# Residual halves of some weights in a two-layer decoder trunk: ScalarE and an accumulating DMA in place of VectorE's subtraction

## Chip, cores and metric

The kernel runs on one core of a Trainium2 chip. The metric is the device time of one execution in microseconds (us). Before the change it is 1392.08 us, the median of 2 runs (1391.61 and 1392.55).

## What is computed

A decoder trunk of two layers on 256 tokens with 2048 channels, all in float32: a retention layer (8 heads), then a multi-scale causal pooling layer, then a last RMS norm.

```python
h = x                                              # (1, 256, 2048)
h = h + retention_layer(h, ret_norm, ret_w_in, ret_gn, ret_w_out)
h = h + pooling_layer(h, pool_norm, pool_w_in, pool_w_grp, pool_b_grp, pool_scale, pool_w_out)
return rms_norm(h, final_norm)

def pooling_layer(...):
    ...
    return (mix * jax.nn.silu(z)) @ w_out          # (256, 4096) @ (4096, 2048)
```

The change lies in that last product, `(mix * silu(z)) @ w_out`, alone.

## The kernel before

TensorE multiplies operands of type float32r, which keep 12 significant bits. So each float32 product a @ b is run as three: a_hi @ b_hi + a_hi @ b_lo + a_lo @ b_hi, where hi is the value rounded to float32r and lo is what the rounding leaves. Every weight therefore has to be split into hi and lo before TensorE can use it.

Weights come in units of 128 partitions x 2048 float32 (1 MB). The helper `weights` (L78 to L91) loads one unit into a tile `raw` by a DMA that SP issues (L81), and splits it in two halves of 1024 columns. For each half ScalarE writes the tile `whi` (a cast, L68) and VectorE writes the tile `wlo` (`raw` minus `whi`, L69). There are three buffers each of `raw`, `whi` and `wlo`. Half n therefore uses the `whi` and `wlo` buffers of half n-3, and ScalarE can't write `whi` of half n before TensorE has ended half n-3.

The last stage is the product with `w_out` (L432 to L487), tokens on partitions. It runs over four column blocks of 512 (`c` from 0 to 3). Each column block takes 8 units (`u` from 0 to 7), so 32 units in all, of two halves each. One half gives 12 matmuls of 512 columns: two row blocks of tokens (`t`), two blocks of channels (`j`), and three products (L442 with `whi`, L443 with `wlo`, L444 with `whi` again). They add up in two accumulators `accy`, one for each `t`. At the end of a column block, for each `t`, VectorE adds the accumulator onto the residual stream (L461), ScalarE squares the sum for the norm (L463), and GpSimd multiplies by the norm's gain (L470). The norm itself and the stores follow after the last column block.

Each engine works its own queue in order. A scheduler lays out the order when the program is built, from the program order, the buffers and its own estimates. GpSimd has little to do in this stage: the multiplications of L470, and ahead of it one load (L420). Its queue is also the one from which accumulating DMAs are issued. In the text below, the halves of an even unit are called a and b, those of the odd unit behind it c and d.

Of the kernel before, what the change touches and what calls it, by code (L numbers as in the profile page):

```python
# [7 lines left out]
F32 = mybir.dt.float32  # L8
# [3 lines left out]
ALU = mybir.AluOpType  # L12

P = 128
D = 2048
S = 256
# [8 lines left out]
EPS = 1e-6  # L25
UNIT = 2048
HALF = UNIT // 2
# [3 lines left out]
def kernel(  # L31
# [15 lines left out]
):  # L47
    """Everything lies transposed, channels on partitions and tokens on the free axis, so that no
    product's result has to be turned; only the retention's values and the last product, which the
    norm of each token follows, have tokens on partitions.  # L50

    A float32 product a @ b runs as a_hi @ b_hi + a_hi @ b_lo + a_lo @ b_hi with float32r operands,
    where hi is the value rounded to the 12 significant bits that TensorE multiplies, and lo, exact
    in float32r, is what the rounding leaves.
    """
    nc = tc.nc
# [7 lines left out]

# [1 line left out]
    def split(hi, lo, src):  # L66
        """hi and lo of src."""
        nc.scalar.copy(hi, src)  # L68
        nc.vector.tensor_tensor(out=lo, in0=src, in1=hi.bitcast(F32), op=ALU.subtract)  # L69

    def split_scaled(hi, lo, src, scale):
        """hi and lo of src times a number for each partition."""
        nc.scalar.activation(hi, src, AF.Identity, scale=scale)
        nc.vector.scalar_tensor_tensor(  # L74
            out=lo, in0=src, scalar=scale, in1=hi.bitcast(F32), op0=ALU.mult, op1=ALU.subtract
        )

    def weights(src, own=None):  # L78
        """Loads a unit of weights and splits it, in two halves, which own has room for if it is given."""
        raw = wpool.tile([P, UNIT], F32, tag="raw", name="raw", bufs=3)  # L80
        nc.sync.dma_start(out=raw, in_=src)  # L81
        halves = []
        for i in range(2):
            if own is None:
                hi = wpool.tile([P, HALF], F32R, tag="whi", name="whi")
                lo = wpool.tile([P, HALF], F32R, tag="wlo", name="wlo")
            else:
                hi, lo = own[:, i, 0], own[:, i, 1]
            split(hi, lo, raw[:, i * HALF : (i + 1) * HALF])
            halves.append((hi, lo))  # L90
        return halves  # L91

    def stationary(acc, blocks, moving):
        """acc[:, :S] + acc[:, S:] = the weights' 128 columns, transposed, times moving."""
        n = len(blocks)
        for k, (hi, lo) in enumerate(blocks):
            nc.tensor.matmul(acc, hi, moving[:, k], start=(k == 0), stop=False)  # L97
            nc.tensor.matmul(acc[:, :S], lo, moving[:, k, 0], start=False, stop=(k == n - 1))  # L98
# [4 lines left out]
    def joined(dst, acc):  # L103
        """The sum of an accumulator's halves."""
        t = ev.tile([P, S], F32, tag="hl", name="hl", bufs=2)
        nc.scalar.copy(t, acc[:, S:])
        nc.vector.tensor_tensor(out=dst, in0=acc[:, :S], in1=t, op=ALU.add)

    def column_sums(sums):
        """Adds up a [P, S] tile over its partitions; every row of the result holds the sums."""  # L110
        sp = ev.tile([P, 2, S], F32R, tag="sp", name="sp", bufs=1)
        split(sp[:, 0], sp[:, 1], sums)
        tot = ps_ret.tile([P, 512], F32, tag="ret", name="tot")
        nc.tensor.matmul(tot[:, :S], ones, sp[:, 0], start=True, stop=False)
        nc.tensor.matmul(tot[:, :S], ones, sp[:, 1], start=False, stop=True)
        return tot[:, :S]

    def rsqrt(dst, a):
        """dst = a ** -0.5, by Newton's steps from a guess on the exponent."""
        n = a.shape[-1]  # L120
        t = ev.tile([P, n], F32, tag=f"rs_t{n}", name="rs_t", bufs=1)
        nc.vector.tensor_scalar(
            out=t.bitcast(I32), in0=a.bitcast(I32), scalar1=1, scalar2=None, op0=ALU.logical_shift_right
        )
        nc.vector.tensor_scalar(
            out=dst.bitcast(I32), in0=t.bitcast(I32), scalar1=-1.0, scalar2=float(0x5F3759DF),
            op0=ALU.mult, op1=ALU.add,
        )
        if n == 1:
            nc.vector.tensor_scalar(out=a, in0=a, scalar1=-0.5, scalar2=None, op0=ALU.mult)  # L130
        for _ in range(3):
            if n == 1:
                nc.vector.tensor_scalar(out=t, in0=dst, scalar1=dst, scalar2=a, op0=ALU.mult, op1=ALU.mult)
                nc.vector.tensor_scalar(out=dst, in0=t, scalar1=1.5, scalar2=dst, op0=ALU.add, op1=ALU.mult)
                continue
            nc.vector.tensor_tensor(out=t, in0=dst, in1=dst, op=ALU.mult)
            nc.vector.scalar_tensor_tensor(out=t, in0=t, scalar=-0.5, in1=a, op0=ALU.mult, op1=ALU.mult)
            nc.vector.scalar_tensor_tensor(out=dst, in0=t, scalar=1.5, in1=dst, op0=ALU.add, op1=ALU.mult)

    def rms(dst, src, scale):  # L140
        """dst = (src * scale + EPS) ** -0.5."""
        a = ev.tile([P, S], F32, tag="rs_a", name="rs_a", bufs=1)
        nc.vector.tensor_scalar(out=a, in0=src, scalar1=scale, scalar2=EPS, op0=ALU.mult, op1=ALU.add)
        rsqrt(dst, a)
# [3 lines left out]

# [1 line left out]
    vec = const.tile([P, 128], F32, name="vec")  # L150
# [6 lines left out]
    nc.scalar.copy(ones, ones_f)  # L157
    # TensorE's clock comes up while the first loads run
    cold = ps_ret.tile([P, 512], F32, tag="ret", name="cold")
# [3 lines left out]

# [1 line left out]
    with tc.tile_pool(name="rt", bufs=1) as rt:  # L165
        xin = act.tile([P, KT * S + 4 * UNIT], F32, tag="os", name="xin")
        raw4 = xin[:, KT * S :].rearrange("p (u f) -> p u f", u=4)
        xin = xin[:, : KT * S].rearrange("p (k s) -> p k s", s=S)
        # the first head's queries and keys, by rows, as the input comes in
        qk = rt.tile([P, 4, S], F32, tag="qk", name="qk")  # L170
# [3 lines left out]
        for u in range(4):  # L174
            raw = raw4[:, u]
# [49 lines left out]
        unit = 4  # L225
        for h in range(NH):
            # queries and keys: the rotation takes their norm with it
            if h:
# [16 lines left out]

            # scores, keys on partitions; the last keys meet the last queries only, [hi | lo] at once
            mk = rt.tile([P, S + P], F32, tag="mk", name="mk", bufs=2)
# [19 lines left out]

            # values, tokens on partitions, less their mean over the head's columns
            accv = [ps_acc.tile([P, 512], F32, tag="acc", name="accv") for _ in range(2)]
# [22 lines left out]

            # what the head gives, centred, and its variance over the head's columns
            o = rt.tile([P, 4, S], F32, tag="tcos", name="o")
# [17 lines left out]

            # gate
            gz = rt.tile([P, 4, S], F32, tag="gz", name="gz")
# [17 lines left out]
    with tc.tile_pool(name="pl", bufs=1) as pl:  # L332
        # the residual stream
        xh = pl.tile([P, KT, S], F32, name="xh")

        # the layer's way out
        hs2 = act.tile([P, KT, 2, S], F32R, tag="hs", name="hs2")
# [19 lines left out]

# [1 line left out]
        gs = act.tile([P, VT, 2, S], F32R, tag="os", name="gs")  # L359
# [10 lines left out]
        for g, win in enumerate(WINDOWS):  # L370
# [3 lines left out]
            for c in range(GT):  # L374
# [3 lines left out]
                u = ubuf[c % 4]  # L378
# [37 lines left out]

        # the residual stream again, tokens on partitions
        last = act.tile([P, 3, D], F32, tag="hs", name="last")
# [8 lines left out]

        # the layer's way out, tokens on partitions, onto the residual stream, and the last norm
        own = pl.tile([P, 2, 2, HALF], F32R, tag="ms", name="own")
        part = pl.tile([P, 2, 4], F32, name="part")  # L430
        base = pl.tile([P, 2], F32, name="base")
        for c in range(4):  # L432
# [14 lines left out]
            for u in range(8):  # L447
                halves += weights(pool_out[8 * c + u], own if (c, u) == (3, 7) else None)
                if c < 3 or u < 6:
                    for half in (2 * u, 2 * u + 1):  # L450
                        rows(half, 0)
                        rows(half, 1)
            if c == 3:
                # the first tokens end ahead of the others
                with tc.manual_schedule(engines={mybir.EngineType.PE}):
                    for t in range(2):
                        for half in range(12, 16):
                            rows(half, t)
# [31 lines left out]
def _layout(inputs):  # L490
    """The arrays as the kernel reads them: the same numbers in another order, and constants."""
    import numpy as np
# [89 lines left out]
```

## Time and profile before

| | |
|---|---|
| median of the runs | 1392.08 us |
| span of the profiled execution | 1391.5 us |
| TensorE busy | 1371.3 us (99%) |
| VectorE busy | 985.4 us (71%) |
| ScalarE busy | 681.3 us (49%) |
| GpSimd busy | 85.3 us (6%) |
| weight loads by SP (`raw`), last stage | 32 of 1 MB, median 4.9 us from issue to landing |

The span is that of one profiled execution; it is 0.6 us under the median of the runs. Busy shares are means over the whole span. To learn what a change in the last stage is worth, one reads that stage by itself: who waits for whom there, and how much time lies between the end of a piece of work and the moment at which TensorE wants it. In the rows below PE is TensorE's matmuls, PEld its weight loads, DVE VectorE, ACT ScalarE, POOL GpSimd and SP the engine that issues most loads. Matmuls overlap in TensorE's pipeline, so a row's duration (0.39 us) is longer than the step from one to the next.

### The profile page before, as it was taken

The numbers are of one execution on the slowest core, as the hardware profiler recorded it, in microseconds if no ns is written. First come the engines' busy times: TensorE is split into PE (matmuls) and PEld (weight loads), VectorE is DVE, ScalarE is ACT, GpSimd is POOL, SyncE is SP. The second block draws the span as 40 slices with busy tenths as digits, with TensorE's granted clock in tenths as the row PEclk, the third lists the DMA queues.
The fourth block names the chain that finished last, engine by engine and source line by source line (L and its number), as shares of the span: only waits on it lengthen the run. The fifth ranks groups of instructions, "written<-read, shape, count | busy, mean of one in ns | idle before, by whom it ended". The sixth has DMA issues, their size and how long they took to land.

```text
span 1391.5 us, 18974 instructions
## 1 busy us (share of the span) xinstructions
PE 1371.3 (99%) x7480; PEld 1185.3 (85%) x7480; DVE 985.4 (71%) x1415; ACT 681.3 (49%) x978; POOL 85.3 (6%) x84
## 2 busy tenths in 40 slices
PE   6999999999999999999999999999999999999997
PEld 5888888888888888888888888888888888888885
DVE  8886868686868686866555867876885896744444
ACT  4554545454545455544444445545454545634443
POOL 7000000000000000012222000000000000000001
PEclk9999999999999999999999999999999999999999
DMA  8455554545454545455555455555555555555552
GB/s 290 156 174 200 176 193 170 195 167 196 167 195 172 185 176 184 179 204 214 195 199 199 176 190 195 193 186 188 195 196 182 189 196 190 205 191 203 187 192 110
DMA packets 39560, 262.70 MB, mean 189 GB/s; under 512 B 4576, under 2 KB 4960, under 8 KB 9136
## 3 DMA queue, kind: packets, MB, share of 16 engines
q1 hardware_dynamic: 37872, 255.93, 52.3%
q0 software_dynamic: 1600, 5.57, 1.1%
q8 instruction: 58, 0.95, 0.3%
q14 instruction: 30, 0.25, 0.0%
HBM read 259.39 MB, written 2.10 MB: 188 GB/s over the span
## 4 chain that ended last, share of the span: by engine, by line
PE 97%; DVE 1%; issue 0%; DMA 0%; SPq 0%; ACT 0%; DVEq 0%; ACTq 0%
PE acc L97 46%; PE acc L98 23%; PE accv L280 4%; PE accv L279 4%; PE accy L444 4%; PE accv L281 4%; PE accy L442 4%; PE accy L443 4%; PE po L299 1%; DVE hs L74 1%; PE po L301 1%; DVE wlo L69 0%; PE acc L197 0%; PE sc L253 0%; PE acc L198 0%
## 5 line engine op out<-in xcount | busy, mean ns | idle before, releaser
L69 DVE TENSOR_TENSOR wlo<-raw,whi 128x1024 fp32r<-128x1024 f32 x470 | 575.3, 1224 | 354.6 <-ACT whi L68 349.6
L68 ACT CAST whi<-raw 128x1024 fp32r<-128x1024 f32 x470 | 494.5, 1052 | 636.1 <-PE acc L97 363.3
L97 PE MATMUL acc<-hs,whi 128*128 128x512 f32 x1984 | 692.8, 393 | 0.0
L98 PE MATMUL acc<-hs,wlo 128*128 128x256 f32 x1984 | 553.8, 279 | 0.0
L97 PEld LDWEIGHTS acc<-hs,whi 128*128 128x128 f32 x1984 | 371.7, 187 | 83.1
L98 PEld LDWEIGHTS acc<-hs,wlo 128*128 128x128 f32 x1984 | 373.9, 188 | 0.9
L97 PE MATMUL acc<-os,whi 128*128 128x512 f32 x512 | 177.5, 394 | 0.0
L98 PE MATMUL acc<-os,wlo 128*128 128x256 f32 x512 | 141.8, 277 | 0.0
L97 PEld LDWEIGHTS acc<-os,whi 128*128 128x128 f32 x512 | 96.0, 188 | 22.3
L280 PE MATMUL accv<-wlo,hs 128*128 128x512 f32 x256 | 99.8, 390 | 0.0
L281 PE MATMUL accv<-whi,hs 128*128 128x512 f32 x256 | 99.6, 390 | 0.0
L443 PE MATMUL accy<-wlo,gs 128*128 128x512 f32 x248 | 96.5, 389 | 0.0
L444 PE MATMUL accy<-whi,gs 128*128 128x512 f32 x248 | 96.5, 389 | 0.0
L98 PEld LDWEIGHTS acc<-os,wlo 128*128 128x128 f32 x512 | 96.1, 188 | 0.0
L279 PE MATMUL accv<-whi,hs 128*128 128x512 f32 x256 | 91.9, 390 | 0.0
L97 PE MATMUL acc<-ms,whi 128*128 128x512 f32 x256 | 90.3, 395 | 0.0
L442 PE MATMUL accy<-whi,gs 128*128 128x512 f32 x248 | 88.0, 389 | 0.0
L98 PE MATMUL acc<-ms,wlo 128*128 128x256 f32 x256 | 71.5, 279 | 0.0
L97 PEld LDWEIGHTS acc<-ms,whi 128*128 128x128 f32 x256 | 48.0, 187 | 11.4
L279 PEld LDWEIGHTS accv<-whi,hs 128*128 128x128 f32 x256 | 48.0, 188 | 10.1
L281 PEld LDWEIGHTS accv<-whi,hs 128*128 128x128 f32 x256 | 48.1, 188 | 9.7
L280 PEld LDWEIGHTS accv<-wlo,hs 128*128 128x128 f32 x256 | 48.1, 188 | 9.4
(141 smaller groups left out, 1135.2 us busy)
## 6 DMA issues: line engine op xcount, KB each, us to landing
raw<-in_ret_in SPq DMA_DIRECT2D x92, 1024.0 KB, 4.9
raw<-in_pool_in SPq DMA_DIRECT2D x64, 1024.0 KB, 4.9
raw<-in_ret_out SPq DMA_DIRECT2D x32, 1024.0 KB, 4.9
raw<-in_pool_out SPq DMA_DIRECT2D x32, 1024.0 KB, 4.9
raw<-in_pool_grp SPq DMA_DIRECT2D x16, 1024.0 KB, 4.9
xin<-in_ret_in SPq DMA_DIRECT2D x7, 512.0 KB, 8.3
xh<-in_xT POOLq DMA_DIRECT2D x8, 256.0 KB, 5.1
out<-last SPq DMA_DIRECT2D x8, 256.0 KB, 2.3
```

What stands on the lines that cost most here:

```text
L68: nc.scalar.copy(hi, src)
L69: nc.vector.tensor_tensor(out=lo, in0=src, in1=hi.bitcast(F32), op=ALU.subtract)
L74: nc.vector.scalar_tensor_tensor(out=lo, in0=src, scalar=scale, in1=hi.bitcast(F32), op0=ALU.mult, op1=ALU.subtract)
L97: nc.tensor.matmul(acc, hi, moving[:, k], start=(k == 0), stop=False)
L98: nc.tensor.matmul(acc[:, :S], lo, moving[:, k, 0], start=False, stop=(k == n - 1))
L279: nc.tensor.matmul(accv[t], hs[:, k, 0, ts], hi[:, ws], start=(k == 0), stop=False)
L280: nc.tensor.matmul(accv[t], hs[:, k, 0, ts], lo[:, ws], start=False, stop=False)
L281: nc.tensor.matmul(accv[t], hs[:, k, 1, ts], hi[:, ws], start=False, stop=(k == KT - 1))
L299: nc.tensor.matmul(po[:, :S], vs[:, 0, p, cs], ss[:, q, :S], start=(n == 0), stop=(n == 2))
L442: nc.tensor.matmul(accy[t], gs[:, k, 0, ts], hi[:, ws], start=(k == 0), stop=False)
L443: nc.tensor.matmul(accy[t], gs[:, k, 0, ts], lo[:, ws], start=False, stop=False)
L444: nc.tensor.matmul(accy[t], gs[:, k, 1, ts], hi[:, ws], start=False, stop=(k == VT - 1))
```

## The change

In the last stage, the odd units of the column blocks 0 and 1 (8 of the 32 units, 16 halves) get their `wlo` in another way. ScalarE casts `whi` as before, then ScalarE writes `wlo` = -`whi`, and then GpSimd issues a DMA that adds the raw weights onto `wlo`. In column block 0 the DMA reads the weights from memory a second time; in column block 1 it reads the tile `raw`. VectorE's subtraction for these halves is gone. All other units are as before. The lines of the changed kernel below `weights` have moved by 6 to 14 numbers: the cast of these halves is L97, the negation L98, the DMA L99, and the matmuls of the stage are L452 to L454.

```diff
-    def weights(src, own=None):
+    def weights(src, own=None, adds=None):
...
-            split(hi, lo, raw[:, i * HALF : (i + 1) * HALF])
+            part = slice(i * HALF, (i + 1) * HALF)
+            if adds is None:
+                split(hi, lo, raw[:, part])
+            else:
+                nc.scalar.copy(hi, raw[:, part])
+                nc.scalar.mul(lo, hi.bitcast(F32), -1.0)
+                nc.gpsimd.dma_start(out=lo, in_=(src if adds == "memory" else raw)[:, part], accum_op=ALU.add)
             halves.append((hi, lo))
...
             for u in range(8):
-                halves += weights(pool_out[8 * c + u], own if (c, u) == (3, 7) else None)
+                halves += weights(
+                    pool_out[8 * c + u],
+                    own if (c, u) == (3, 7) else None,
+                    {0: "memory", 1: "loaded"}.get(c) if u % 2 else None,
+                )
```

On ScalarE's queue, from the start of the second odd unit of column block 0, the rows before are only casts (the numbers are those of the buffers as the program names them):

```order
L68 CAST whi_11105<-raw_11103 128x1024
L68 CAST whi_11109<-raw_11103 128x1024
L68 CAST whi_11139<-raw_11137 128x1024
L68 CAST whi_11143<-raw_11137 128x1024
L68 CAST whi_11173<-raw_11171 128x1024
L68 CAST whi_11177<-raw_11171 128x1024
```

and now, for the same halves (a, b, c, d, and a, b of the next pair):

```order
L68 CAST whi_11107<-raw_11105 128x1024
L68 CAST whi_11111<-raw_11105 128x1024
L97 CAST whi_11141<-raw_11139 128x1024
L98 ACTIVATE wlo_11142<-whi_11141 128x1024
L97 CAST whi_11146<-raw_11139 128x1024
L98 ACTIVATE wlo_11147<-whi_11146 128x1024
L68 CAST whi_11177<-raw_11175 128x1024
L68 CAST whi_11181<-raw_11175 128x1024
```

Each negation stands directly behind the cast of its half, and the casts of the next even unit stand behind both.

On ScalarE's queue at the turn from column block 0 to column block 1, the rows before are (`sqn` is the square at a column block's end, first for `t` 0, then for `t` 1):

```order
L68 CAST whi_11319<-raw_11317 128x1024
L68 CAST whi_11323<-raw_11317 128x1024
L68 CAST whi_11353<-raw_11351 128x1024
L463 ACTIVATE sqn_11308,part_11031<-last_10980 128x512
L463 ACTIVATE sqn_11312,part_11031<-last_10980 128x512
L68 CAST whi_11357<-raw_11351 128x1024
L68 CAST whi_11387<-raw_11385 128x1024
```

and now:

```order
L68 CAST whi_11327<-raw_11325 128x1024
L68 CAST whi_11331<-raw_11325 128x1024
L477 ACTIVATE sqn_11316,part_11031<-last_10980 128x512
L97 CAST whi_11361<-raw_11359 128x1024
L477 ACTIVATE sqn_11320,part_11031<-last_10980 128x512
L98 ACTIVATE wlo_11362<-whi_11361 128x1024
L97 CAST whi_11366<-raw_11359 128x1024
L68 CAST whi_11397<-raw_11395 128x1024
L98 ACTIVATE wlo_11367<-whi_11366 128x1024
L68 CAST whi_11401<-raw_11395 128x1024
```

Both squares now stand ahead of the negation of half c (`wlo_11362`), and the cast of the next unit's first half (`whi_11397`) stands ahead of the negation of half d (`wlo_11367`).

On GpSimd's queue the end of the program before is:

```order
L373 DMA ic_7801<-in_icnt 128x256
L373 DMA ic_8853<-in_icnt 128x256
L373 DMA ic_9913<-in_icnt 128x256
L420 DMA last_10980<-in_g_last 128x2048
L470 TENSOR_TENSOR last_10980<-last_10980 128x512 x7
```

and now, from the last two accumulating DMAs of column block 0 on:

```order
L99 DMA wlo_11282<-in_pool_out 128x1024
L99 DMA wlo_11287<-in_pool_out 128x1024
L484 TENSOR_TENSOR last_10980<-last_10980 128x512 x2
L99 DMA wlo_11362<-raw_11359 128x1024
L99 DMA wlo_11367<-raw_11359 128x1024
```

The two multiplications that end column block 0 stand ahead of the first DMA of column block 1.

## Rows read from the trace of the kernel before

**Rows 1.** The profile's page, chain that ended last, by engine.

```profile
PE 97%; DVE 1%; issue 0%; DMA 0%; SPq 0%; ACT 0%; DVEq 0%; ACTq 0%
```

**Rows 2.** Waits of TensorE over the whole span: us in total, times, longest.

```profile
PE acc L198 <- DVE wlo L69: 7.6, 6, 1.8
PE acc L197 <- ACT whi L68: 2.1, 3, 1.0
```

**Rows 3.** Waits of all engines in the last stage, 1215 to 1392 us.

```profile
ACT whi L68 <- PE accy L444: 88.1, 56, 1.7
DVE wlo L69 <- ACT whi L68: 78.0, 54, 2.9
```

**Rows 4.** Timeline in the last stage: start us, us, instruction, [idle before <-releaser].

```profile
1259.15 0.61 PE L442 MATMUL accy<-whi,gs 128*128 128x512 f32 x2
...
1261.87 0.61 PE L442 MATMUL accy<-whi,gs 128*128 128x512 f32 x2
1262.07 1.05 ACT L68 CAST whi<-raw 128x1024 fp32r<-128x1024 f32 x1 [1.67 <-PE accy L444]
...
1263.15 1.22 DVE L69 TENSOR_TENSOR wlo<-raw,whi 128x1024 fp32r<-128x1024 f32 x1 [1.49 <-ACT whi L68]
...
1264.59 0.61 PE L442 MATMUL accy<-whi,gs 128*128 128x512 f32 x2
```

**Rows 5.** Groups of instructions by line, 1170 to 1392 us: busy us, mean ns.

```profile
L69 DVE TENSOR_TENSOR wlo<-raw,whi 128x1024 fp32r<-128x1024 f32 x73 | 89.4, 1225 | 89.2 <-ACT whi L68 88.6
L68 ACT CAST whi<-raw 128x1024 fp32r<-128x1024 f32 x73 | 77.0, 1055 | 102.3 <-PE accy L444 88.5 <-PE acc L97 9.3 <-issue 4.2
```

**Rows 6.** DMA issues by line: count, KB each, median us from issue to landing.

```profile
raw<-in_pool_out SPq DMA_DIRECT2D x32, 1024.0 KB, 4.9
...
xh<-in_xT POOLq DMA_DIRECT2D x8, 256.0 KB, 5.1
...
last<-in_g_last POOLq DMA_DIRECT2D x1, 1024.0 KB, 7.6
...
rp<-in_rope POOLq DMA_DIRECT2D x1, 256.0 KB, 2.9
...
idt<-in_ident POOLq DMA_DIRECT2D x1, 64.0 KB, 2.4
```

**Rows 7.** Busy time by stretch: stage of the `xh` loads and last stage (clock, DMA share, GB/s last).

```profile
596.00:741.00 145.00, 145.00 (x838) 126.75 (x838) 87.16 (x101) 64.57 (x82) 35.46 (x34) 1.00 0.57 202
1215.00:1380.00 165.00, 165.00 (x729) 136.55 (x728) 79.07 (x81) 66.78 (x73) 10.14 (x7) 1.00 0.51 179
```

**Rows 8.** Timeline at the turn from column block 0 to 1.

```profile
1250.70 1.28 DVE L461 TENSOR_TENSOR last<-last,accy 128x512 f32<-128x512 f32 x2
...
1251.19 1.06 ACT L68 CAST whi<-raw 128x1024 fp32r<-128x1024 f32 x1 [1.67 <-PE accy L444]
1252.15 0.62 ACT L463 ACTIVATE sqn<-last 128x512 f32<-128x512 f32 x1
...
1252.67 0.19 ACT L463 ACTIVATION_READ_ACCUMULATOR sqn<-last 128x1 f32 x1
```

**Rows 9.** Timeline of GpSimd, 1150 to 1392 us, same columns.

```profile
1252.95 2.95 POOL L470 TENSOR_TENSOR last<-last 128x512 f32<-128x512 f32 x2 [68.04 <-ACT sqn L463]
```

**Rows 10.** Timeline of TensorE in the first stage, 22 to 42 us, same columns.

```profile
26.87 0.74 PE L198 MATMUL acc<-hs,wlo 128*128 128x256 f32 x4 [1.79 <-DVE wlo L69]
...
27.80 0.39 PE L197 MATMUL acc<-hs,whi 128*128 128x512 f32 x1
...
28.14 0.39 PE L197 MATMUL acc<-hs,whi 128*128 128x512 f32 x1
...
31.71 1.03 PE L198 MATMUL acc<-hs,wlo 128*128 128x256 f32 x4 [1.78 <-DVE wlo L69]
32.53 0.63 PE L197 MATMUL acc<-hs,whi 128*128 128x512 f32 x1
...
33.17 0.63 PE L197 MATMUL acc<-hs,whi 128*128 128x512 f32 x1
```

**Rows 11.** Busy time by stretch there; third value from the end is the granted clock.

```profile
32.00:33.00 1.00, 1.00 (x6) 0.90 (x6) 1.00 (x2) 0.00 (x0) 1.00 (x2) 0.50 0.67 115
35.00:36.00 1.00, 1.00 (x6) 0.88 (x5) 1.00 (x2) 0.88 (x1) 0.00 (x0) 0.82 0.19 75
```

## The prediction

> **What bounds the kernel now.** I read the chain that ended last first: TensorE holds 97% of it, VectorE 1% [rows 1]. Then the waits of TensorE itself: over the whole span it waits for VectorE 7.6 us and for ScalarE 2.1 us, longest wait 1.8 us [rows 2]. Rows 10 show where such waits lie: in the first stage. In the last stage the list of waits has ScalarE waiting for TensorE (88.1 us in 56 waits) and VectorE for ScalarE (78.0 us), and no row in which TensorE waits [rows 3]. So in the stage that is changed TensorE never runs short, and ScalarE and VectorE are held by it through the three buffers.
>
> The timeline gives the margin. TensorE starts halves at 1259.15, 1261.87 and 1264.59: 2.72 us each, 0.227 for each of 12 matmuls [rows 4]. At 1262.07, 0.20 after the half that it waits for has ended, ScalarE casts (1.05 us), and VectorE subtracts from 1263.15 to 1264.37 [rows 4]. Call 1261.87 time 0. The half made here has number n, the one that TensorE has just begun n-2. Its `wlo` is there at 2.50, and TensorE needs it after two more halves and the matmuls with `whi` that stand ahead (one or two; two in the odd units): at 2 x 2.72 + 2 x 0.227 = 5.89. The margin is 3.4 us, and all of the change has to fit into it.
>
> **What the change removes.** 16 subtractions of 1.225 us [rows 5], 19.6 us of VectorE. They end 3.4 us before they are wanted and nothing behind them is wanted earlier, so removing them gives nothing. Bounds: 0, and at most the 1% of the chain that VectorE holds over the whole program, hardly any of it here.
>
> **What it adds, by pair of units (a, b with subtraction, c, d with the DMA).** Half c: cast from 0.20 to 1.25, negation of the same 1024 columns, taken as long as the cast, 1.055 us [rows 5], to about 2.35, and 0.05 until GpSimd issues: 2.4. Then the DMA, L us from issue to landing. `wlo` of c is ready at 2.4 + L, wanted at 5.89. TensorE waits L - 3.5.
>
> Half d: its buffers are free when TensorE ends a, at 2.72, so its cast runs from 2.92, its DMA starts at 5.1 and lands at 5.1 + L. TensorE, late by c, wants it at 2.4 + L + 10 x 0.227 + 0.45 = 5.12 + L. So d waits for nothing more as long as both transfers take the same. ScalarE's 2.1 us in an odd half lie inside the 2.72. Each pair loses L - 3.5 once, and there are 8 pairs.
>
> **L.** No row shows an accumulating DMA. Plain ones that GpSimd issued: 64 KB in 2.4 us and 256 KB in 2.9 us alone in the first stage; beside the weight loads 256 KB take 5.1 us and 1024 KB take 7.6 us [rows 6]. The DMA engines are busy 0.57 in the stage of the 5.1 us row and 0.51 in ours [rows 7], so the busy rows are the ones to go by. A half is 512 KB. Lower end: a plain 512 KB alone, from the two quiet rows 2.9 + 256 x 0.5 / 192 = 3.6 us. Plain and beside loads: 5.1 + 256 x 2.5 / 768 = 5.9 us. But an add onto the destination must read the destination as well as the source: 1024 KB read, 512 KB written, which leans to the 7.6 us row. Upper end: 7.6 and 2.5 more (what 768 KB more cost in these rows) for the neighbour half's accumulation in flight: 10.1 us. I take the middle of 5.9 and 7.6, 6.8 us, the rows nearest to it, and keep 3.6 and 10.1.
>
> Waits: 8 x (6.8 - 3.5) = 26.4 us, with ends 0.8 and 53.
>
> The Trainium skill, DMA: Bandwidth & Descriptors, section on the anatomy of one DMA on the SWDGE path, gives a fit of 2.0 us plus bytes over 436 KB per us for such a transfer; an estimate from it is 3.2 us for a half, and the waits would be gone. The row for 256 KB beside loads, 5.1 us against 2.6 by the fit, does not agree with it [rows 6].
>
> **The turn from column block 0 to 1.** Here the order has moved ScalarE's two squares ahead of the negation of c, and GpSimd's two multiplications ahead of its DMA. From the rows at this place [rows 8, 9], with the column block's last half ending at 1250.99 (0.20 before the cast): VectorE's two additions end near 1251.34 and 1251.98, the first square (0.62 + 0.19, slightly overlapped, 0.75) ends near 1252.1, the cast near 1253.1, the second square near 1253.8, the negation near 1254.8. The two multiplications (2.95 us together) end near 1255.25. The DMA starts at 4.25 instead of 2.4: 1.85 us more of wait. For d, the cast of the next unit stands ahead of the negation and waits for TensorE to end b, at 5.44; cast and negation follow, the DMA starts at 7.8, lands at 7.8 + L, and is wanted at 4.25 + L + 2.72 = 6.97 + L: 0.85 more. Together 2.7 us, once.
>
> **The clock.** TensorE has never stood still for over 1.8 us before. In the first stage it waits 1.79 us and goes on at full speed (two products 0.34 us apart), then 1.78 us, and goes on with 0.64 us for the same two products [rows 10]; the granted clock is 0.50, the 1.2 GHz level, from 32 us until about 35.4 (0.82 in the second from 35) [rows 11]. In these 3.4 us it did what takes 1.8 at 2.4 GHz: a fall costs 1.6 us. Waits of 3.3 us are longer than both. Bounds: no fall (0), and one in each of 8 waits (12.6 us). I take 6 of 8: 9.4 us.
>
> The Trainium skill, TensorE: Matmul & The Clock Gate, section on HAM oscillation, tells of a kernel in which each wait for a load sends the clock down, so that every tile starts slow; an estimate by it is all eight, 12.6 us instead of 9.4. The row with 1.79 us, after which the clock stayed, shows that not every wait does.
>
> **What else moves.** In column block 1, `raw` of an odd unit is held until d's DMA has landed, at 5.1 + L = 11.9. SP's next load into it takes 4.9 us, to 16.8, and its first reader is the cast that waits for TensorE to begin c of the next pair, past 14 + 5.4 = 19.6. The margin is 2.8 us; it costs nothing, or 1 to 2 us in four units if L is over 9. The second read in column block 0 is 4 MB more from memory, in the DMA time already counted.
>
> **Sum.** 26.4 + 2.7 + 9.4 = 38.5 us. On the profiled execution's span of 1391.5 and the 0.6 us between it and the median: 1392.1 + 38.5 = 1430.6; I say 1430.
>
> **Rivals.** (1) *The transfer is hidden.* If the DMA lands within 3.5 us, TensorE meets `wlo` in time in 7 of 8 pairs; the turn alone costs its 2.7 us or less: about 1394, not slower. It is decided at L = 3.5. For it: quiet transfers of 256 KB take 2.9 us, and the DMA engines are idle half of the time [rows 6, 7]. Against: 256 KB took 5.1 us beside the same loads, and this is twice as much with another read. (2) *Short waits at full clock.* L of 5.1 to 5.9 gives waits of 1.6 to 2.4 us, after which the clock may stay as it did at 1.79 [rows 10]: 8 x 2 + 2.7 = 19, about 1411. For it: 512 KB read on the average row. Against: the second read. (3) *The accumulation is slow*, or c's and d's DMAs share the engines and take each other's time: L = 10.1 gives 8 x 6.6 + 2.7 + 12.6 = 68, 1460, and d would wait behind c as well. For it: nothing in the trace has ever added in a DMA. Against: the DMA engines have half their time free [rows 7]. (4) *A gain*, because VectorE is relieved: against it rows 1 to 3, nothing for it. That the change doesn't do what it says I leave out: the order shows the 16 DMAs.
>
> **How the numbers follow.** Forecast (L of 6 to 8.5, clock falls in most waits) 0.50; hidden 0.10; short waits at full clock 0.21; slow accumulation 0.18; gain 0.01. The range of 8 in 10 leaves out the hidden case and the far end of the slow one: low 1404 (L = 4.7 without the clock: 8 x 1.2 + 2.7 = 12), high 1464 (L = 10.1 with some wait of d). 2% of 1392, about what a measurement of this kernel tells from no change, is 28 us: 1420. Slower by over 2%: the forecast, the slow case and a bit of the short one, 0.70. Within 2%: the hidden case and most of the short one, 0.29. Faster by over 2%: 0.01.
>
> **What would show it.** In the profile after, TensorE's first matmul with `wlo` of each odd unit (L453) waits for the DMA, 8 times some 3.3 us, and hardly at all for d; at the turn 5 to 6 us. The DMA rows of L99 show L: near 6.8 is right, at 3.5 or less the forecast falls. The granted clock dips to 0.50 in the two column blocks and nowhere in the last two. VectorE's busy time is 20 us less, ScalarE's 17 us more. Column blocks 2 and 3 take 43.5 us each as before. If the time lost lies on ScalarE's queue or on SP's loads instead of the DMA's landing, my reason is wrong even if the sum is right.

## The result and the profile after

The changed kernel takes 1431.65 us (1431.09 and 1432.22) against 1392.08: 1.0288 times the time of before, 95% interval 1.0271 to 1.0305. It is slower by 39.6 us. The forecast was 1430, slower, with 1404 to 1464 as its range.

The profile's page, busy time by engine, then the DMA queues (packets, MB, share of 16 engines), the chain by engine, and the group of the products with `wlo`:

```profile
PE 1386.5 (97%) x7480; PEld 1192.7 (83%) x7480; DVE 966.5 (68%) x1399; ACT 697.1 (49%) x994; POOL 98.4 (7%) x100
...
q1 hardware_dynamic: 37872, 255.93, 50.5%
q0 software_dynamic: 3904, 13.96, 4.2%
...
PE 92%; DMA 4%; issue 1%; DVE 1%; SPq 1%; ACT 1%; POOL 0%; DVEq 0%; POOLq 0%; ACTq 0%
...
L453 PE MATMUL accy<-wlo,gs 128*128 128x512 f32 x248 | 102.9, 415 | 24.1 <-DMA wlo<-in_pool_out 15.3
...
wlo<-in_pool_out POOLq DMA_DIRECT2D x8, 512.0 KB, 6.9
wlo<-raw POOLq DMA_DIRECT2D x8, 512.0 KB, 4.7
```

Three things are to be seen. TensorE's share of the chain has gone from 97% to 92% [rows 1], and DMA is now in the chain. The products with `wlo`, which never waited, wait 24.1 us, all of it for the accumulating DMAs. And TensorE is busy 15.2 us longer (1371.3 before) with the same 7480 matmuls: the same work, for the most part at a lower clock. VectorE is 18.9 us less busy, ScalarE 15.8 us more, close to what the instructions taken away and added come to.

The busy time by stretch shows where. The stretches are column blocks 0, 1 and 2 (PE, PEld, DVE, ACT, POOL; then clock, DMA share, GB/s):

```profile
1206.70:1275.40 68.70, 53.44 (x194) 40.95 (x193) 12.75 (x15) 25.82 (x27) 6.99 (x8) 0.88 0.71 184
1275.40:1333.20 57.80, 48.98 (x193) 38.80 (x192) 11.13 (x10) 26.22 (x28) 9.47 (x10) 0.91 0.76 205
1333.20:1376.70 43.50, 43.50 (x193) 36.03 (x192) 21.22 (x20) 18.11 (x20) 3.27 (x2) 1.00 0.58 211
```

Block 2 takes 43.5 us, as every block did. Block 0, which adds from memory, takes 25.2 us more and block 1, which adds from `raw`, 14.3 more: together 39.5, all of the loss. The mean clock (1.00 is 2.4 GHz) says how long the lower level of 0.50 (1.2 GHz) was granted: 2 x 0.12 x 68.7 = 16.5 us in block 0, 2 x 0.09 x 57.8 = 10.4 in block 1. In these 26.9 us at half speed TensorE loses at most 13.5. With the 24.1 us of waits that is 37.6; the last 2 us are the ends of the 11 matmuls ahead of a wait, whose rows (0.39 us) are longer than the step of 0.23.

The second odd unit of block 0 in the timeline (rows of c and d; start us, us, instruction, [idle before <-releaser]):

```profile
1225.71 1.05 ACT L97 CAST whi<-raw 128x1024 fp32r<-128x1024 f32 x1 [5.19 <-PE accy L454]
1226.79 1.06 ACT L98 ACTIVATE wlo<-whi 128x1024 fp32r<-128x1024 f32 x1
1228.15 0.87 POOL L99 DMA_DIRECT2D wlo<-in_pool_out  x1 [13.42 <-ACT wlo L98]
1228.66 1.05 ACT L97 CAST whi<-raw 128x1024 fp32r<-128x1024 f32 x1 [0.81 <-PE accy L454]
1229.74 9.38 SPq L85 DMA_DIRECT2D raw<-in_pool_out  x2
1229.75 1.06 ACT L98 ACTIVATE wlo<-whi 128x1024 fp32r<-128x1024 f32 x1
1231.10 0.86 POOL L99 DMA_DIRECT2D wlo<-in_pool_out  x1 [2.09 <-ACT wlo L98]
...
1233.82 0.50 PE L453 MATMUL accy<-wlo,gs 128*128 128x512 f32 x1 [2.02 <-DMA wlo<-in_pool_out]
...
1239.97 0.80 PE L453 MATMUL accy<-wlo,gs 128*128 128x512 f32 x1 [3.09 <-DMA wlo<-in_pool_out]
```

Cast, negation, DMA, landing stand behind each other as forecast: c's DMA starts 2.4 us after the start of the cast and lands 5.6 us later, and TensorE has waited 2.0 us. What was not forecast is d: its DMA starts 1.4 us after SP's next load of 1 MB, which starts as soon as d's cast has read `raw`, and needs 8.8 us, and TensorE waits again, 3.1 us. In these microseconds the DMA engines are full (last but one value):

```profile
1230.00:1239.00 9.00, 4.85 (x20) 3.31 (x19) 2.45 (x2) 2.90 (x3) 0.86 (x1) 1.00 0.98 224
```

The list of TensorE's waits has both sources of the accumulating DMA (us in total, times, longest):

```profile
PE accy L453 <- DMA wlo<-in_pool_out: 15.3, 7, 3.1
PE accy L453 <- DMA wlo<-raw: 8.8, 4, 3.5
```

From `raw` there are 4 waits, one for each c and none for d; from memory 7, so d waits in 3 of 4 pairs.

### The profile page after: what moved, and what is told of

Its sections match the earlier page's. It is cut to its first block, busy times and chain, and to the rows that moved or that the text cites. A ratio compares the mean times of both kernels' runs of the same rounds, so it can differ in the third digit from the quotient of the medians.

```text
span 1430.5 us, 19024 instructions
## 1 busy us (share of the span) xinstructions
PE 1386.5 (97%) x7480; PEld 1192.7 (83%) x7480; DVE 966.5 (68%) x1399; ACT 697.1 (49%) x994; POOL 98.4 (7%) x100
## 3 DMA queue, kind: packets, MB, share of 16 engines
q1 hardware_dynamic: 37872, 255.93, 50.5%
## 4 chain that ended last, share of the span: by engine, by line
PE 92%; DMA 4%; issue 1%; DVE 1%; SPq 1%; ACT 1%; POOL 0%; DVEq 0%; POOLq 0%; ACTq 0%
PE acc L107 44%; PE acc L108 23%; PE accv L290 4%; PE accv L289 4%; PE accv L291 4%; PE accy L453 3%; PE accy L454 3%; PE accy L452 3%; DMA wlo<-in_pool_out 2%; DMA wlo<-raw 1%; PE po L309 1%; DMA xin<-in_ret_in 1%; PE po L311 1%; PE acc L207 0%; DVE wlo L69 0%
## 5 line engine op out<-in xcount | busy, mean ns | idle before, releaser
L69 DVE TENSOR_TENSOR wlo<-raw,whi 128x1024 fp32r<-128x1024 f32 x454 | 556.2, 1225 | 406.7 <-ACT whi L68 401.7
L68 ACT CAST whi<-raw 128x1024 fp32r<-128x1024 f32 x454 | 477.4, 1052 | 628.0 <-PE acc L107 362.1
L107 PE MATMUL acc<-hs,whi 128*128 128x512 f32 x1984 | 692.8, 393 | 0.0
L453 PE MATMUL accy<-wlo,gs 128*128 128x512 f32 x248 | 102.9, 415 | 24.1 <-DMA wlo<-in_pool_out 15.3
L454 PE MATMUL accy<-whi,gs 128*128 128x512 f32 x248 | 101.5, 409 | 0.0
L452 PE MATMUL accy<-whi,gs 128*128 128x512 f32 x248 | 93.5, 407 | 0.0
L453 PEld LDWEIGHTS accy<-wlo,gs 128*128 128x128 f32 x248 | 49.3, 199 | 39.4 <-DMA wlo<-in_pool_out 18.5
L452 PEld LDWEIGHTS accy<-whi,gs 128*128 128x128 f32 x248 | 49.4, 199 | 11.0
L454 PEld LDWEIGHTS accy<-whi,gs 128*128 128x128 f32 x248 | 49.6, 200 | 10.4
```

The lines of the kernel that those rows point to most:

```text
L452: nc.tensor.matmul(accy[t], gs[:, k, 0, ts], hi[:, ws], start=(k == 0), stop=False)
L453: nc.tensor.matmul(accy[t], gs[:, k, 0, ts], lo[:, ws], start=False, stop=False)
L454: nc.tensor.matmul(accy[t], gs[:, k, 1, ts], hi[:, ws], start=False, stop=(k == VT - 1))
```

## The experiments

Theory: the landing of the accumulating DMA, later than the three buffers leave room for, makes TensorE wait, and the waits bring the clock down. Rivals: the longer work and the other order on ScalarE; the place (the first column block) rather than the source; the DMA engines' time as the limit.

**e2_vector_adds: the DMA alone undone.**

```diff
-                nc.gpsimd.dma_start(out=lo, in_=(src if adds == "memory" else raw)[:, part], accum_op=ALU.add)
+                nc.vector.tensor_tensor(out=lo, in0=raw[:, part], in1=lo.bitcast(F32), op=ALU.add)
```

> ScalarE's negation stays, but VectorE adds raw onto it; no accumulating DMA. Theory 'the DMA's landing is the cost': wlo of c is ready at 2.4 + 1.3 = 3.7 us, inside the 5.9, so no waits in the stage and 1392 to 1394 us. Rival 'the longer work and the changed order on ScalarE are a cost': 8 waits of 0.5 us or more, 1397 us or over.

Measured 1392.11 us, 0.9999 of before (0.9990 to 1.0009). Block 0 in the profile:

```profile
1207.40:1250.90 43.50, 43.50 (x194) 36.03 (x193) 22.35 (x23) 25.91 (x27) 0.00 (x0) 1.00 0.56 194
```

ScalarE works 25.9 us here, as long as in the changed kernel (25.8), and TensorE doesn't wait. ScalarE's added work costs nothing; the whole 39.6 us hang on the DMA.

**e1_swapped: the sources change places.**

```diff
-                    {0: "memory", 1: "loaded"}.get(c) if u % 2 else None,
+                    {0: "loaded", 1: "memory"}.get(c) if u % 2 else None,
```

> The two sources change places: column block 0 adds from the tile raw, column block 1 from memory. In the changed kernel block 0 (memory) took 68.7 us and block 1 (raw) 57.8, against 43.5 before. Theory 'source': the length goes with the source, about 57 us for block 0 and 69 for block 1, the DMAs from memory again 5.7 us (c) and 8.7 us (d) to landing, those from raw 4.5 to 5.7 us; total 1428 to 1436. Rival 'place': the first column block is the dear one whatever it reads, because its DMAs start from the pooling stage: block 0 stays near 69 us and block 1 near 58.

Measured 1432.6 us (1430.17 and 1435.03). Blocks 0 and 1:

```profile
1205.60:1260.60 55.00, 47.94 (x194) 38.05 (x193) 12.72 (x15) 25.86 (x27) 6.97 (x8) 0.94 0.80 216
1260.60:1331.10 70.50, 50.73 (x193) 39.01 (x193) 11.25 (x11) 26.21 (x28) 9.51 (x10) 0.88 0.72 190
```

The long block goes with the source: 55.0 us from `raw`, 70.5 from memory. The place is not the cause. The total came out between the 1428 and 1436 us expected.

**e6_held and e8_held_at_end: why memory is dearer.** In the "memory" units a small GpSimd addition behind half d reads `raw` and `wlo`, so that SP can't load into `raw` before d's DMA has landed.

```diff
+                if adds == "memory" and i == 1:
+                    kept = ev.tile([P, 1], F32, tag="kept", name="kept", bufs=1)
+                    nc.gpsimd.tensor_tensor(out=kept, in0=raw[:, :1], in1=lo[:, :1].bitcast(F32), op=ALU.add)
```

> In column block 0 (adds from memory) a [128 x 1] GpSimd addition reads raw and wlo after half d's DMA has landed, so that SP's next weight load can't start before that, as it is in block 1 (adds from raw). Theory 'contention': d's 8.7 us comes from the weight load that starts 1.4 us before it; held back, d's DMA lands in 4.5 to 6 us and block 0 takes 56 to 60 us instead of 68.7, total 1419 to 1424. Rival 'memory is the slow source': d stays above 8 us, block 0 stays at 66 us or over, total 1429 or over.

Measured 1435.07 us: a miss for the total, though block 0 took 57.8 us. The stages ahead of it were 13 us longer, though nothing of the edit runs there. In this kernel the tile `kept` stands in the pool `ev`, and the tiles allocated behind it had moved (by 32 bytes; the traces hold no addresses that show it). So `kept` was put at the end of the last pool:

> As e6_held, but the [128 x 1] tile is the last one in its pool, so that no other tile changes its address. e6_held took 57.8 us for block 0 as the theory 'contention' has it, but its earlier stages were 13 us longer. Theory 'address': those 13 us came from the tiles that the small tile had moved by 32 bytes; here they are gone, block 0 takes 56 to 60 us, total 1419 to 1424. Rival 'the extra GpSimd work itself': total stays at 1430 or more.

Measured 1421.82 us. Block 0 and the landing times:

```profile
1207.20:1267.50 60.30, 48.82 (x194) 38.36 (x194) 12.46 (x15) 25.88 (x27) 7.78 (x12) 0.92 0.75 195
...
wlo<-in_pool_out POOLq DMA_DIRECT2D x8, 512.0 KB, 5.9
wlo<-raw POOLq DMA_DIRECT2D x8, 512.0 KB, 4.6
```

Block 0 is down from 68.7 to 60.3 us and the landing from memory from 6.9 to 5.9, with no value above 7.6 where it was 8.8. The 13 us are gone: this kernel and e6_held have the same instructions in the same order on every engine, and differ in the place of `kept` alone. So some 8 of the 11 us by which the block from memory was longer than the one from `raw` (68.7 and 57.8) were the weight load that starts beside d's DMA; with `raw` as the source that load can't start, because `raw` is still being read. Some 1.3 us at landing stay with memory as the source.

**e9_spare: the 32 bytes alone**, in the kernel before.

```diff
+    spare = ev.tile([P, 1], F32, tag="spare", name="spare", bufs=1)
+    nc.gpsimd.memset(spare, 0.0)
```

> The kernel before with one [128 x 1] tile more, cleared once at the start and never read; it moves the tiles allocated after it by 32 bytes. Theory 'address': as in e6_held, longer stages from the first on, 1400 to 1408 us. Rival 'not the address': 1392 within 1 us.

Measured 1397.61 us, 1.0044 (1.0027 to 1.0061). Slower as the theory has it, though below the 1400 to 1408 us that it gave. Every engine has its instructions in the same order as before, but for the one that clears the tile. The costliest matmul group, first of e9_spare, then of e6_held, then of the kernel before:

```profile
L100 PE MATMUL acc<-hs,whi 128*128 128x512 f32 x1984 | 698.7, 396 | 0.0
```

```profile
L110 PE MATMUL acc<-hs,whi 128*128 128x512 f32 x1984 | 701.8, 398 | 0.0
```

```profile
L97 PE MATMUL acc<-hs,whi 128*128 128x512 f32 x1984 | 692.8, 393 | 0.0
```

In the changed kernel and in e8_held_at_end it is 692.8 us and 393 ns too. By the order of the pools in the kernel, the tiles that this group names stand where they stood. Which of the moved tiles slows it, and how, stays open.

**e3_plain_copy: the same DMAs without the addition.**

```diff
-                ... in_=(src if adds == "memory" else raw)[:, part], accum_op=ALU.add)
+                ... in_=(src if adds == "memory" else raw)[:, part])
```

> The same 16 DMAs copy the raw weights over wlo without adding (left out: the addition; wlo then holds the whole weight). It prices the accumulation itself. Theory 'reading the destination makes it long': from memory 4.5 us for c and 6.5 for d, from raw 3.6 us, total 1408 to 1418. Rival 'the add is nearly free, a GpSimd transfer of 512 KB costs this much anyway': times to landing within 0.5 us of those with the add, total 1427 to 1433.

Measured 1414.49 us. The queue of the DMAs that GpSimd issues, in the kernel before and in this one, and this one's landing times:

```profile
q0 software_dynamic: 1600, 5.57, 1.1%
...
q0 software_dynamic: 3904, 13.96, 2.8%
...
wlo<-in_pool_out POOLq DMA_DIRECT2D x8, 512.0 KB, 4.6
wlo<-raw POOLq DMA_DIRECT2D x8, 512.0 KB, 3.1
```

So the addition is dear. From `raw` a landing takes 3.1 us in the median instead of 4.7, from memory 4.6 instead of 6.9. The queue's share gives the engine time: 1.1% of 1391.5 us before is 15.3 us; 2.8% of 1413.8 is 39.6, so 24.3 for 16 plain copies, 1.5 us each; 4.2% of 1430.5 is 60.1, so 2.8 us for each accumulation. The queue that SP's loads use moved 255.93 MB, 244 times 1024 KB, in 50.5% of 1430.5: 3.0 us for a weight load of 1 MB. An accumulation of 512 KB occupies the DMA engines nearly as long as a load of twice the bytes. The Trainium skill, Collectives: The Full Stack, section on the bandwidth ceiling, says of the add in a reduce-scatter that it halves the rate because of the second source that it reads; 2.8 against 1.5 us agrees in size, but no run here parts that read from the adding.

**e7_filled: the clock.** 72 idle matmuls, whose result nobody reads, in TensorE's waits.

```diff
+                if c < 2 and u % 2:
+                    for hi, _ in halves[-2:][: 2 - c]:
+                        warm = ps_ret.tile([P, 512], F32, tag="ret", name="warm")
+                        for _ in range(6):
+                            nc.tensor.matmul(warm, gs[:, 0, 0, :P], hi[:, :512], start=True, stop=True)
```

> The changed kernel with idle matmuls (128 x 512, into a PSUM tile that nobody reads) ahead of the first product with wlo in the odd units: 12 in block 0 and 6 in block 1, 72 in all, 16 us of TensorE's work at full speed, placed inside its waits. Theory 'the low clock is a cost of its own' (15 us more TensorE busy time in the changed kernel): nearly no stretch at 0.50 in the two blocks, and although 16 us of work is added the total falls, to 1418 to 1427. Rival 'what the low clock costs would else be waited out for the same landings': total stays at 1430 or more, or grows by the added work.

Measured 1427.69 us (1425.15 and 1430.23), between the two: 4.0 us under the changed kernel, though the two runs lie 5 us apart. Blocks 0 and 1:

```profile
1207.40:1275.40 68.00, 59.08 (x242) 47.05 (x242) 12.81 (x15) 25.87 (x27) 6.99 (x8) 0.95 0.72 186
1275.40:1331.20 55.80, 50.52 (x217) 40.15 (x216) 11.13 (x10) 26.26 (x28) 9.48 (x10) 1.00 0.77 212
```

The clock stays up (1.00 in block 1, where it was 0.91; 0.95 in block 0, from 0.88), and with 72 x 0.227 = 16.3 us more work the two blocks are 2.7 us shorter. So the waits do bring the clock down. But the 13.5 us that TensorE lost to it do not come back: beside the idle matmuls it still waits 14.2 us for the accumulating DMAs, 30.5 us together where it was 24.1. The same landings are then waited for. By this one experiment a few us of the loss are the clock's own; most of it is the landing's either way.

**e4_ahead: the landing taken off the buffers.** ScalarE writes -round(`raw`) from `raw` into four buffers of the tile `own`, and the DMA adds onto that, ahead of the even unit's split. The cast of `whi` comes later.

```diff
+        def ahead(c, u):
...
+                lo = own[:, u // 2 % 2, i]
...
+                nc.scalar.mul(lo, raw[:, part], -1.0)
+                nc.gpsimd.dma_start(
+                    out=lo, in_=(pool_out[8 * c + u] if c == 0 else raw)[:, part], accum_op=ALU.add
+                )
...
+                        made = ahead(c, u + 1)
```

> For the same 8 units the residual is made ahead: ScalarE writes -round(raw) straight from raw into 4 buffers of its own (the tile own, free until the last unit), in the program before the even unit's split, and the DMA adds raw onto it; whi is cast later, when its buffer is free. The DMA's landing is no longer tied to the three whi and wlo buffers. Theory 'the margin of 5.9 us behind the buffers is what turned the landing into waits': TensorE's waits for the DMA are gone or under 3 us in all, the clock stays at 1.00, 1392 to 1396 us, the change then neither gains nor loses. Rival 'the 16 transfers slow the weight loads or the DMA engines are the bound': waits remain, now for raw or for the DMA, 1403 us or more.

Measured 1407.79 us, 1.0114 (1.0097 to 1.0131): 24 of the 39.6 us are gone, some 15 stay. TensorE's waits for the accumulations have fallen from 24.1 to 2.4 us, all in the first unit, so the margin behind the buffers was the cause of the rest. In their place:

```profile
PE accy L475 <- ACT whi L68: 3.1, 3, 2.5
PE accy L476 <- DMA own<-in_pool_out: 2.4, 1, 2.4
PE accy L476 <- DVE wlo L69: 1.5, 3, 0.8
PE accy L475 <- ACT whi L459: 1.4, 1, 1.4
...
1205.60:1255.80 50.20, 46.82 (x195) 37.04 (x194) 10.17 (x13) 25.49 (x28) 8.32 (x10) 0.97 0.90 252
1255.80:1307.40 51.60, 46.56 (x192) 36.56 (x192) 13.03 (x13) 24.50 (x28) 8.20 (x9) 0.97 0.89 244
```

TensorE now waits for the casts and subtractions behind weight loads that come late (up to 11.6 us to landing), and the DMA engines are busy 0.90. A pair of units wants 2 x 3.0 + 2 x 2.8 = 11.6 us of them, TensorE only 10.9. By this they have become the bound; 8 times these 0.7 us are 5.6 of the 15 us, and the rest was not worked out. That they are the bound was tried:

**e10_ahead_half: the same for 4 units** (u of 3 and 7).

> As e4_ahead, but for 4 units (u of 3 and 7 in column blocks 0 and 1) in place of 8. By the queue's share in the profile an accumulating DMA of 512 KB keeps the DMA engines busy 2.8 us, a weight load of 1 MB 3.0; a pair of units then wants 2 x 3.0 + 2 x 2.8 = 11.6 us of them, and TensorE needs only 10.9 for it. Theory 'the DMA engines became the bound in e4_ahead': over two pairs it is now 17.6 of 21.8 us, nothing is left of the loss, 1392 to 1395 us. Rival 'making it ahead costs something else (raw held longer, ScalarE's order)': half of e4_ahead's 15 us, 1398 or more.

Measured 1394.19 us, 1.0016 (1.0007 to 1.0025). Blocks 0 and 1, then the waits for the accumulations:

```profile
1205.20:1250.10 44.90, 43.98 (x194) 35.92 (x193) 17.46 (x20) 21.39 (x23) 3.53 (x4) 1.00 0.78 235
1250.10:1295.10 45.00, 44.10 (x193) 35.96 (x193) 15.74 (x16) 21.66 (x24) 6.44 (x6) 1.00 0.77 234
...
PE accy L476 <- DMA own<-in_pool_out: 0.9, 1, 0.9
PE accy L476 <- DMA own<-raw: 0.9, 1, 0.9
```

With the DMA engines at 0.78 nearly all of the loss is gone, where half of e4_ahead's 15 us was expected if the DMA engines were not the bound, and the clock never falls in the two blocks. It still gains nothing: VectorE's relief has no taker. No version here beats the kernel before.

## Why the prediction was right

*What bounds the kernel.* Right: the kernel with all of ScalarE's added work and no DMA (e2_vector_adds) takes 1392.1 us, so TensorE's 97% and its waits [rows 1 to 3] told that nothing else was near. The 19 us taken from VectorE gained nothing in any run.

*The margin.* Right. The DMA of c starts 2.4 us after the start of the cast (2.2 forecast). With the measured L of each c, L - 3.5 gives its wait to within 0.2 us, but for the turn: 2.0 to 2.5 us from memory, 1.4 to 2.4 from `raw`. And e4_ahead shows that the waits go when the start is freed from the buffers.

*L.* The single value of 6.8 us was the middle of what turned out to be three: 4.7 us from `raw`, 5.6 for c from memory, and 7.9 to 8.8 for d from memory. That an accumulation is dearer than a plain copy holds: 2.8 us of the engines against 1.5. The reason given, that an add reads its destination too, fits this but no run shows it by itself.

*Where the waits lie.* The step that failed is "d waits for nothing more as long as both transfers take the same". From memory they don't: in that mode `raw` is free as soon as it is cast, SP's load starts beside d's DMA, and both are slowed (e8_held_at_end). I had put the second read "in the DMA time already counted" and had not asked when SP's load would start. The sign that I had given, 8 waits of some 3.3 us and hardly any for d, didn't come: c waited less, and d three times, 6.1 us in all. Waits forecast: 26.4 us and 2.7 at the turn, 29.1. Measured: 24.1.

*The turn from block 0 to 1.* The order did there what the rows of the order told: the squares and the multiplications pushed c's DMA to some 5 us behind the block's end (4.25 forecast), and d's to 7.9 (7.8 forecast). TensorE waited 3.5 us instead of 5.2, since L was 4.6.

*The clock.* Right that it falls; 9.4 us forecast, 13.5 at most measured. It fell at seven of the eleven waits, of 1.8, 2.3, 2.3, 2.4, 2.5, 3.1 and 3.5 us, once for twice as long as else, and not at the four of 1.2, 1.4, 1.5 and 2.0 us. I had counted six falls. As a term of a sum it was put too simply: e7_filled shows that most of what the low clock costs would be waited for anyway.

*The sum.* Forecast 29.1 and 9.4, measured 24.1 and 13.5 and 2 us of matmul ends: the terms missed by 4 to 5 us each and nearly cancel. That the total is right to 2 us is luck; the sign and the mechanism are what the runs bear out.

*The rivals.* Hidden transfers need L of 3.5: a plain copy from `raw` would have come to that (3.1 us), an accumulation doesn't. Short waits were the common case: L was 4.5 to 5.9 us in 12 of the 16 transfers, at or under what that rival took, but the clock did not stay up behind them. Slow accumulation happened for d from memory alone.

## What to carry to other kernels

Before work is moved from an engine to a DMA, ask not whether the DMA engines have time left but how long the work takes from its first input to its landing, and set that against the time that the buffers leave between "free" and "wanted"; here 5.9 us had to hold two ScalarE passes and a landing. An accumulating DMA costs the DMA engines about twice a plain copy of the same bytes. Ask of every transfer what else will start when it frees its source: the cheaper-looking mode, which let `raw` go early, was the dearer one, because the next load then ran beside it and filled the DMA engines for 9 us, which their mean share of 0.71 in that block doesn't show.

## What the runs showed that I had not expected

In block 0 a load of 1 MB and d's accumulation of 512 KB start 1.4 us apart, while c's accumulation is under way. d's DMA landed after up to 8.8 us instead of c's 5.6, and SP's load, 4.9 us in the median of the stage, was as late in the same pairs. The engine times account for it: 2.8 + 3.0 + 2.8 = 8.6 us for the three, and the DMA engines were busy 0.98 of the 9 us from 1230 to 1239. DMA engines that are idle for half of the stage before can so be the limit for the few us in which a landing is wanted.

```profile
DMA to landing us min/median/max: 4.8/6.0/8.9
```

(that row: SP's weight loads of the changed kernel between 1210 and 1275 us.)

GpSimd's issue of an accumulating DMA takes 0.86 us in its row; the plain copy of the same bytes in e3_plain_copy takes 0.53, and the loads of before 0.53 to 0.58, but for one of 0.74. So the addition lengthens the issue on the engine as well, by 0.33 us.

One more tile of [128 x 1], which moves the tiles allocated behind it, made matmuls slower that by the order of the pools use none of the moved tiles: 393 to 396 and 398 ns in the mean, 0.4% of the kernel's time in e9_spare and some 13 us in e6_held. An experiment that adds a tile should therefore put it where nothing else moves.
